# A hybrid decoder block on one core: value products, their sum, and the gates' second half move within the units of the mix stage, and four attention blocks start a unit later

## The chip, the cores and the metric

The kernel runs on one core of a Trainium2 chip. The metric is the device time of one execution in microseconds (us); the figure for a kernel is the median of its runs. TensorE (PE) does the matrix products, VectorE (DVE), ScalarE (ACT) and GpSimd (POOL) the elementwise work, SyncE (SP) issues the weight loads. Each engine works through its own queue in order and waits there for what it needs from others.

## The reference

One decoder block over 512 tokens and 16 learned meta tokens, width 1024, in float32: a SwiGLU, then attention and a state-space layer side by side, merged by sigmoid gates, then a second SwiGLU.

```python
h = h + 0.5 * swiglu(rmsnorm(h, ffn1_norm), w1, w3, w2)
q, k, v, u, g_attn, g_ssm = jnp.split(rmsnorm(h, mix_norm) @ w_in, SPLITS, axis=-1)
attn = sliding_window_attention(q, k, v, attn_sinks)   # 16 heads, 4 of keys and values, window 128, 16 meta keys, a sink per head
y = jax.nn.gelu(s5_ssm(u, ...))
ssm = (y @ ssm_glu_a) * jax.nn.sigmoid(y @ ssm_glu_b)
merged = jax.nn.sigmoid(g_attn) * attn + jax.nn.sigmoid(g_ssm) * ssm
h = h + merged @ w_out
h = h + 0.5 * swiglu(rmsnorm(h, ffn2_norm), ...)
return rmsnorm(h, final_norm)[:, N_META:]
```

## The kernel before

Activations lie transposed, features on partitions and the 512 tokens along the row. Every float32 operand of a large product is split into a high and a low part (`hi`, `lo`), and each product is done as three: hi by hi, hi by lo, lo by hi. The weights come in by SP's queue, are split by ACT (`whi`, L173) and DVE (`wlo`, L174), and are used a *unit* at a time: a unit is one tile of 128 output columns, 8 chunks of 128 rows by three products, so 24 matmuls of 128x512 (L238) into one PSUM bank.

The change lies in the mix stage, 30 units that stand in the order of the table `MIX`: the remaining query columns (`q`), the gates of attention (`ga`) and of the state-space layer (`gs`), and the two halves of its output (`glu`, "value-gate units": a unit with two banks, 12 products for the half `b`, then 12 for `a`). Unit 4 is the first `glu`, unit 9 the second `ga`, unit 15 the last `q`.

The attention runs between the products of these units. It is cut into 16 blocks b0 to b15: block n is key head n // 4 with 128 query rows n % 4, four query heads at once. A block takes three units:

- `s1` in its first unit, once for each of four heads: a *score pair* on PE (L1167, L1168, into one of two score banks), the masked minimum on DVE (L1170: writes `E`, `mn` and frees the bank), the exp on ACT (L1172). After the fourth head come the sums `den` on DVE, and POOL multiplies `E` by 1/`den` (L1183).
- `s2o`, `s2p`, `s2m` in the next unit: PE transposes `E` (L1191), ACT and DVE split it (`ph`, `pl`); the meta keys' part is transposed (L1210), split into `ms`, and POOL spreads it over the heads as `m` (`m4` in the code, L1215).
- `s3` in the third unit: the *value products* (L1226, four, or two where n % 4 is 0) into the only value bank `pv`; `s3m`: the *sum product* with the meta values (L1234), which needs `m`; `s3e`: the *sum of the halves*, hi part and lo part of the values: ACT copies one half (`tb`, L1240), DVE adds the other into `AT` (L1242, twice), which frees the bank.

Where each of these stands in a unit is written by hand. A unit of 24 products has 11 cuts: cut j comes before product 2(j + 1). In a `glu` unit cuts 0 to 5 fall into the first half (before its products 1, 3, 5, 6, 8, 10) and 6 to 10 into the second (before 2, 4, 6, 8, 10). `BEGIN` holds the unit in which each block starts, `CUT` the cut of each step. What a unit leaves in its bank is taken up at cut 0 of the next (`flush`). The next weight tile is prepared at cut 8 (`prep_piece`). No scheduler changes this order afterwards: the engines' queues are filled as the code runs.

```python
if i - 2 in begin:
    for f, c in ((s3, "s3"), (s3m, "s3m"), (s3e, "s3e")):
        at_cut(CUT[c], f, begin[i - 2])
if i in begin:
    for h in range(4):
        at_cut(CUT["s1"][h], s1, begin[i], h)
if i - 1 in begin:
    for f, c in ((s2o, "s2o"), (s2p, "s2p"), (s2m, "s2m")):
        at_cut(CUT[c], f, begin[i - 1])
```

Of the kernel before, what the change touches and what calls it, by code (L numbers as in the profile page):

```python
# [10 lines left out]
AF = mybir.ActivationFunctionType  # L11
ALU = mybir.AluOpType
# [25 lines left out]
PREPS = (6, 34)  # L38
KS1 = 8
VS = (1, 0, 2, 10, 13, 13)  # L40
CUT = {"s3": 5, "s3m": 7, "s3e": 9, "s1": (2, 4, 7, 7), "s2o": 7, "s2p": 7, "s2m": 8, "prep": 8, "ev": 0, "ks": 10, "vs": 7}
BEGIN = (1, 2, 3, 4, 6, 7, 10, 11, 13, 14, 15, 18, 19, 20, 21, 24)

NG = 32
NST = 64
# [20 lines left out]
def hybrid_block_kernel(  # L66
# [30 lines left out]
    V, S, G, PE, SY = nc.vector, nc.scalar, nc.gpsimd, nc.tensor, nc.sync  # L97
# [13 lines left out]
    def real(t):  # L111
        return t.rearrange("p (h c) -> p h c", h=2)[:, :, :256]
# [79 lines left out]
    def step(mm, evac, hold=False, mids=(), prep=True):  # L192
        hi, lo = take()
        mm(hi, lo, mids)
        if prep:
            prep_piece()
        pend.append(evac)
        if not hold:
            flush()
# [31 lines left out]
    def mm3(outs, hi, lo, rhi, rlo, nk, mids, k0=0):  # L231
        seq = []
        for k in range(nk):
            seq += [(hi, rhi, k), (hi, rlo, k), (lo, rhi, k)]

        def emit(w, r, k, start, stop):
            for o, sl in outs:
                PE.matmul(out=o, lhsT=w[:, k0 + k, :], rhs=sl(r, k), start=start, stop=stop)  # L238

        accumulate(seq, emit, mids)  # L240
# [10 lines left out]
    def mm512(ps, hi, lo, rhi, rlo, nk, mids, k0=0, packed=True):  # L251
        if packed:
            mm3([(ps, lambda r, k: r[:, k, :])], hi, lo, rhi, rlo, nk, mids, k0)
        else:
            mm3([(ps, lambda r, k: real(r[:, k, :]))], hi, lo, rhi, rlo, nk, mids, k0)
# [48 lines left out]
    def new_hg(cols=COLS, p=hg_p):  # L304
        hi = p.tile([128, ND, cols], F32R, tag="hgh", name="hgh")
        lo = p.tile([128, ND, cols], F32R, tag="hgl", name="hgl")
        return hi, lo
# [720 lines left out]
    def h2(t):  # L1028
        return t.rearrange("p (h c) -> p h c", h=2)

    def unit512(evac_f):
        cell = {}

        def mm(hi, lo, mids):
            cell["p"] = mm_ps.tile([128, 512], F32, tag="mm", name="p")
            mm512(cell["p"], hi, lo, hg[0], hg[1], ND, mids, packed=False)
        return mm, lambda: evac_f(h2(cell["p"]))
# [47 lines left out]
    AT = a_p.tile([128, ND, SEQ], F32, name="AT")  # L1085
# [4 lines left out]
    def tmp(name):  # L1090
        return a_p.tile([128, 512], F32, tag="t", name=name, bufs=4)
# [157 lines left out]
    def merge(m):  # L1249
        V.scalar_tensor_tensor(out=AT[:, m, :], in0=gst.pop(m), scalar=0.5, in1=AT[:, m, :], op0=ALU.mult, op1=ALU.add)  # L1250
        if m >= 6:
            msplit(m)

    def ev_ga(m):
        def f(p):
            t = tmp("ta")
            V.tensor_tensor(out=h2(t), in0=p, in1=r512, op=ALU.mult)
            S.activation(out=t, in_=t, func=AF.Tanh, scale=0.5)
            V.scalar_tensor_tensor(out=AT[:, m, :], in0=t, scalar=1.0, in1=AT[:, m, :], op0=ALU.add, op1=ALU.mult)
            if m < 6:  # L1260
                merge(m)
        return f

    def ev_gs(m):
# [7 lines left out]
    def unit_glu(m):  # L1272
        cell = {}

        def mm(hi, lo, mids):
            n = (len(mids) + 1) // 2
            for key, k0, ms in (("b", 4, mids[:n]), ("a", 0, mids[n:])):
                cell[key] = mm_ps.tile([128, 512], F32, tag="mm", name="p")
                mm512(cell[key], hi, lo, YH, YL, 4, ms, k0)

        def ev():
            t = tmp("tg")
            S.activation(out=t, in_=cell["b"], func=AF.Tanh, scale=0.5)
            V.scalar_tensor_tensor(out=t, in0=t, scalar=1.0, in1=cell["a"], op0=ALU.add, op1=ALU.mult)
            V.scalar_tensor_tensor(out=gst[m], in0=gst[m], scalar=1.0, in1=t, op0=ALU.add, op1=ALU.mult)
            if m >= 6:
                merge(m)
        return mm, ev
# [3 lines left out]
    def msplit(m):  # L1292
        S.activation(out=mg[0][:, m, :], in_=AT[:, m, :], func=AF.Copy)
        V.tensor_tensor(out=mg[1][:, m, :], in0=AT[:, m, :], in1=fr(mg[0][:, m, :]), op=ALU.subtract)
# [5 lines left out]
    for kind, r in MIX:  # L1300
        for m in (2 * r, 2 * r + 1):
            units.append(unit_glu(m) if kind == "glu" else unit512({"q": ev_q, "ga": ev_ga, "gs": ev_gs}[kind](m)))
    begin = dict(zip(BEGIN, range(16)))
    for i, u in enumerate(units):
        cuts = [[] for _ in range(NCUT)]

        def at_cut(c, f, *a):
            cuts[c].append(lambda: f(*a))
# [8 lines that stand above are left out]
            for f, c in ((s2o, "s2o"), (s2p, "s2p"), (s2m, "s2m")):  # L1317
                at_cut(CUT[c], f, begin[i - 1])
        at_cut(CUT["ev"], flush)
        if i == KS1:  # L1320
            at_cut(CUT["ks"], ksplit, 1)
            at_cut(CUT["ks"], vmeta, 1)
        for v, iv in enumerate(VS):
            if i == iv:
                at_cut(CUT["vs"], vsplit, *divmod(v, 3))
        at_cut(CUT["prep"], prep_piece)
        if i == len(units) - 2:
            mg += new_hg(SEQ)
            for m in range(6):
                at_cut(m, msplit, m)  # L1330

        step(*u, mids=[lambda fs=fs: [f() for f in fs] for fs in cuts], prep=False, hold=i < len(units) - 1)
# [170 lines left out]
```

## Time and profile before

| | |
|---|---|
| median of 3 runs | 1147.18 us (1145.42 to 1149.43) |
| the profiled execution | 1148.62 us, its span 1146.80 us |
| busy in the span: PE, PE weight loads | 1127.8 us (98%), 1006.2 us (88%) |
| busy: DVE, ACT, POOL | 636.5 (55%), 410.4 (36%), 357.1 us (31%) |
| chain that ended last | PE 88%, DVE 5%, ACT 4%, issue 2%, DMA 1% |
| matmuls in L238 | 403.6 + 403.1 + 401.2 us, 1408 of each kind |

A row of the profile in order of time reads: start, duration, engine, line, operation, output <- inputs, shape, and in brackets how long the engine had been idle and what ended that. Matmuls overlap, so their spacing and not their duration tells PE's pace. A row of the waits reads: engine and operation that waited, what it waited for, us in total, times, the longest. A row of stretches has the stretch, its length, the busy time of PE, its weight loads, DVE, ACT and POOL, then the granted clock of PE, the DMA share and GB/s.

### The profile page before, as it was taken

The page shows a single profiled execution, that of the slowest core. Times are in us where ns is not written, and L with a number is a line of the kernel's source. Part 1 is how long each engine was busy: PE and PEld are TensorE (multiplying, and loading weights), DVE is VectorE, ACT ScalarE, POOL GpSimd, SP SyncE. Part 2 cuts the span into 40 slices and gives each one's busy share as a digit, 9 for nine tenths or more (in the row PEclk, how much of TensorE's full clock was granted, in tenths as well). Part 3 has the DMA queues.
Part 4 walks back from the last instruction along what each step waited for, and adds up shares of the span by engine and source line. Part 5 has one row for each costly group of instructions (what it writes and reads, how often), then busy time and mean ns, then how long its engine had stood idle before and what let it go on. Part 6 is the DMA issues. An engine that isn't in the chain of part 4 may idle for free.

```text
span 1146.8 us, 17241 instructions
## 1 busy us (share of the span) xinstructions
PE 1127.8 (98%) x7006; PEld 1006.2 (88%) x7006; DVE 636.5 (55%) x960; ACT 410.4 (36%) x727; POOL 357.1 (31%) x488
## 2 busy tenths in 40 slices
PE   9999999999999999999999999999999999999997
PEld 7999999999999999977778778888888888888887
DVE  5446663655444464867767776664544444444454
ACT  5322232232222242465646554443322321322234
POOL 1966663542883030444444231020000000000003
PEclk7999999999999999999999999999999999999999
DMA  5423233232423246212211222432423224313222
GB/s 164 115 94 110 74 94 112 75 85 84 112 87 95 77 160 170 56 63 74 74 58 53 74 74 81 144 106 74 129 92 111 74 83 127 111 65 128 75 74 74
DMA packets 105583, 108.43 MB, mean 95 GB/s; under 512 B 7504, under 2 KB 101968, under 8 KB 105376
## 3 DMA queue, kind: packets, MB, share of 16 engines
q1 hardware_dynamic: 103104, 100.74, 28.0%
q0 software_dynamic: 2352, 6.52, 2.2%
q8 instruction: 55, 0.90, 0.3%
q14 instruction: 24, 0.20, 0.1%
q10 hardware_dynamic: 48, 0.07, 0.0%
HBM read 100.80 MB, written 5.34 MB: 93 GB/s over the span
## 4 chain that ended last, share of the span: by engine, by line
PE 88%; DVE 5%; ACT 4%; issue 2%; DMA 1%; POOL 0%; SPq 0%; DVEq 0%; POOLq 0%; ACTq 0%
PE p L238 59%; PE p L412 11%; PE p L414 9%; PE p L800 2%; PE pv L1226 1%; PE p L1398 1%; DVE wlo L174 1%; ACT whi L173 1%; PE ps_t L1191 1%; DVE AT L1242 1%; PE ps_s L1167 1%; ACT E L1172 1%; PE ps_s L1168 1%; DMA xb<-in_x_dram 1%; ACT qs L1144 0%
## 5 line engine op out<-in xcount | busy, mean ns | idle before, releaser
L238 PE MATMUL p<-hgh,whi 128*128 128x264 f32 (+1 forms) x1408 | 403.6, 333 | 0.1
L238 PE MATMUL p<-hgl,whi 128*128 128x264 f32 (+1 forms) x1408 | 403.1, 332 | 0.0
L238 PE MATMUL p<-hgh,wlo 128*128 128x264 f32 (+1 forms) x1408 | 401.2, 331 | 0.0
L174 DVE TENSOR_TENSOR wlo<-raw,whi 128x1024 fp32r<-128x1024 f32 (+2 forms) x192 | 257.7, 1342 | 91.6 <-ACT whi L173 89.4
L238 PEld LDWEIGHTS p<-hgh,whi 128*128 128x128 f32 x1408 | 238.9, 188 | 26.0 <-issue 0.8
L238 PEld LDWEIGHTS p<-hgh,wlo 128*128 128x128 f32 x1408 | 238.6, 189 | 23.5
L238 PEld LDWEIGHTS p<-hgl,whi 128*128 128x128 f32 x1408 | 238.9, 188 | 22.4
L173 ACT ACTIVATE whi<-raw 128x1024 fp32r<-128x1024 f32 (+2 forms) x192 | 187.5, 979 | 133.5 <-PE p L414 72.2
L1414 POOL TENSOR_TENSOR acc<-acc,zq 128x256 f32<-128x256 f32 x12 | 8.9, 738 | 349.8 <-ACT zq L1407 349.7
L432 DVE SCALAR_TENSOR_TENSOR hT<-p,hT 128x528 f32<-128x528 f32 (+1 forms) x56 | 39.1, 698 | 87.1 <-PE p L414 52.2
L384 ACT ACTIVATE t<-t 128x528 f32<-128x528 f32 (+1 forms) x44 | 28.1, 639 | 165.0 <-DVE t L383 164.9
L394 ACT ACTIVATE gh<-t 128x528 fp32r<-128x528 f32 (+1 forms) x44 | 28.1, 639 | 160.6 <-DVE t L393 160.6
L412 PE MATMUL p<-gh,whi 128*128 128x264 f32 x352 | 72.6, 288 | 0.7 <-DVE hT L432 0.5
L412 PE MATMUL p<-gl,whi 128*128 128x264 f32 x352 | 71.5, 284 | 0.0
L412 PE MATMUL p<-gh,wlo 128*128 128x264 f32 x352 | 71.4, 284 | 0.0
L383 DVE TENSOR_TENSOR t<-p,r_bc 128x528 f32<-128x528 f32 (+1 forms) x44 | 30.7, 698 | 71.3 <-PE p L238 68.1
L393 DVE TENSOR_TENSOR t<-p,t 128x528 f32<-128x528 f32 (+1 forms) x44 | 30.7, 698 | 65.4 <-PE p L238 65.0
L412 PEld LDWEIGHTS p<-gh,whi 128*128 128x128 f32 x352 | 54.5, 189 | 1.9 <-issue 0.8
L414 PE MATMUL p<-gh,whi 128*128 128x512 f32 x144 | 56.0, 389 | 0.0
L414 PE MATMUL p<-gl,whi 128*128 128x512 f32 x144 | 56.0, 389 | 0.0
L414 PE MATMUL p<-gh,wlo 128*128 128x512 f32 x144 | 56.0, 389 | 0.0
L385 DVE TENSOR_TENSOR t<-t,r_bc 128x528 f32<-128x528 f32 (+1 forms) x44 | 37.2, 846 | 32.4 <-ACT t L384 32.4
(322 smaller groups left out, 1502.2 us busy)
## 6 DMA issues: line engine op xcount, KB each, us to landing
raw<-in_ffn_w_dram SPq DMA_DIRECT2D x42, 1024.0 KB, 5.4
raw<-in_ffn_w_dram SPq DMA_DIRECT2D x24, 768.0 KB, 4.3
raw<-in_w_in_dram SPq DMA_DIRECT2D x16, 1024.0 KB, 5.5
raw<-in_ffn_w_dram SPq DMA_DIRECT2D x12, 512.0 KB, 3.6
raw<-in_w_out_dram SPq DMA_DIRECT2D x4, 1024.0 KB, 8.1
h_keep<-hT POOLq DMA_DIRECT2D x1, 2112.0 KB, 7.3
raw<-in_ssm_glu_a_dram SPq DMA_DIRECT2D x4, 512.0 KB, 3.6
raw<-in_ssm_glu_b_dram SPq DMA_DIRECT2D x4, 512.0 KB, 5.3
```

The source lines that it names most:

```text
L173: S.activation(out=hi, in_=src, func=AF.Copy)
L174: V.tensor_tensor(out=lo, in0=src, in1=fr(hi), op=ALU.subtract)
L238: PE.matmul(out=o, lhsT=w[:, k0 + k, :], rhs=sl(r, k), start=start, stop=stop)
L383: V.tensor_tensor(out=t1, in0=cell[1], in1=rb(), op=ALU.mult)
L384: S.activation(out=t1, in_=t1, func=AF.Silu)
L385: V.tensor_tensor(out=t1, in0=t1, in1=rb(), op=ALU.mult)
L393: V.tensor_tensor(out=t3, in0=cell[3], in1=cell["t1"], op=ALU.mult)
L394: S.activation(out=gh, in_=t3, func=AF.Copy)
L412: PE.matmul(out=p[:, h, :HALF], lhsT=wt[:, k, :], rhs=gs[k][c][:, h, :], start=start, stop=stop)
L414: PE.matmul(out=p, lhsT=wt[:, k, :], rhs=gs[k][c].rearrange("p h c -> p (h c)"), start=start, stop=stop)
L432: V.scalar_tensor_tensor(out=hv(hT, d), in0=cell["p"], scalar=0.5, in1=hv(hT, d), op0=ALU.mult, op1=ALU.add)
L800: PE.matmul(out=p[:, h, :HALF], lhsT=w[:, k, :], rhs=r[:, k, h * HALF:(h + 1) * HALF], start=(n == 0), stop=(n == 3 * ND - 1))
```

## The change

The value products go from cut 5 to cut 1, the sum product from 7 to 3, the sum of the halves from 9 to 5. The second half of an attention gate (two DVE operations, L1259 and L1250) no longer follows its first half at cut 0 but is kept back (`pend2`) to cut 6. The tanh of a value-gate unit is issued as soon as its half `b` is done, no longer with the rest at the next unit's cut 0. Blocks b0 to b3 start in units 2 to 5 in place of 1 to 4; the other twelve stay.

```diff
-CUT = {"s3": 5, "s3m": 7, "s3e": 9, "s1": (2, 4, 7, 7), ...}
-BEGIN = (1, 2, 3, 4, 6, 7, 10, 11, 13, 14, 15, 18, 19, 20, 21, 24)
+CUT = {"s3": 1, "s3m": 3, "s3e": 5, "ev2": 6, "s1": (2, 4, 7, 7), ...}
+BEGIN = (2, 3, 4, 5, 6, 7, 10, 11, 13, 14, 15, 18, 19, 20, 21, 24)
...
+    pend2 = []
+
+    def flush2():
+        while pend2:
+            pend2.pop(0)()
...
     def ev_ga(m):
...
             S.activation(out=t, in_=t, func=AF.Tanh, scale=0.5)
-            V.scalar_tensor_tensor(out=AT[:, m, :], in0=t, scalar=1.0, in1=AT[:, m, :], op0=ALU.add, op1=ALU.mult)
-            if m < 6:
-                merge(m)
+
+            def second():
+                V.scalar_tensor_tensor(out=AT[:, m, :], in0=t, scalar=1.0, in1=AT[:, m, :], op0=ALU.add, op1=ALU.mult)
+                if m < 6:
+                    merge(m)
+            pend2.append(second)
...
     def unit_glu(m):
...
                 mm512(cell[key], hi, lo, YH, YL, 4, ms, k0)
+                if key == "b":
+                    t = cell["t"] = tmp("tg")
+                    S.activation(out=t, in_=cell["b"], func=AF.Tanh, scale=0.5)
 
         def ev():
-            t = tmp("tg")
-            S.activation(out=t, in_=cell["b"], func=AF.Tanh, scale=0.5)
+            t = cell["t"]
...
         at_cut(CUT["ev"], flush)
+        at_cut(CUT["ev2"], flush2)
```

In the queues, the numbers behind the names tell one buffer from another. PE in unit 15, where b10 is scored, b9 transposed and b8 summed, before: around b8's value products and sum product.

```order
L1167 MATMUL ps_s_6892<-KH_5678,qs_6264 128x272
L1168 MATMUL ps_s_6892<-KL_5679,qs_6264 128x272
L238 MATMUL p_6865<-hgl_213,whi_6769 128x512
L238 MATMUL p_6865<-hgh_212,wlo_6770 128x512
L1226 MATMUL pv_6899<-ph_6842,VB_5680 128x512
L1226 MATMUL pv_6899<-pl_6843,VB_5680 128x512
```

And after, the same products of the same block:

```order
L238 MATMUL p_6865<-hgh_212,whi_6775 128x512
L1226 MATMUL pv_6877<-ph_6842,VB_5680 128x512
L1226 MATMUL pv_6877<-pl_6843,VB_5680 128x512
L238 MATMUL p_6865<-hgl_213,whi_6775 128x512
L238 MATMUL p_6865<-hgh_212,wlo_6776 128x512
L1167 MATMUL ps_s_6886<-KH_5678,qs_6254 128x272
L1168 MATMUL ps_s_6886<-KL_5679,qs_6254 128x272
```

Before, two score pairs and 12 products of the unit stand ahead of the value products; after, 4 products and no pair. The sum product follows four products later in both.

DVE in the same unit, before: the end of b10's scores (`E` and `mn` of the fourth head), the rest of its unit, and then b8's sum of the halves.

```order
L1170 ISA E_6879,mn_6880<-ps_s_6912,mC_5684,sinkn_67 128x272
L1170 ISA mn_6880 128x1
L1175 TENSOR_TENSOR es_6882<-mn_6880,sinkn_67 128x4
L1177 TENSOR_TENSOR den_6881<-den_6881,es_6882 128x4
L1178 RECIPROCAL den_6881<-den_6881 128x4
L1181 TENSOR_TENSOR pm_6921<-E_6879,den_6881 128x64
L1195 TENSOR_TENSOR pl_6931<-ps_t_6925,ph_6930 128x512
L1195 TENSOR_TENSOR pl_6940<-ps_t_6934,ph_6939 128x512
L1213 TENSOR_TENSOR ms_6947<-ps_tm_6945,ms_6947 64x128
L174 TENSOR_TENSOR wlo_6953<-raw_6623,whi_6952 128x1024
L1242 TENSOR_TENSOR AT_5682<-pv_6899,tb_6961 64x2x128 x2
```

And after, from the second head's score on:

```order
L1170 ISA E_6882,mn_6883<-ps_s_6896,mC_5684,sinkn_67 128x272
L1170 ISA mn_6883 128x1
L1242 TENSOR_TENSOR AT_5682<-pv_6877,tb_6903 64x2x128 x2
L1170 ISA E_6882,mn_6883<-ps_s_6911,mC_5684,sinkn_67 128x272
L1170 ISA mn_6883 128x1
```

The additions into `AT` went from behind `wlo`, the last work of the unit, to between the second and the third head's score.

POOL at b2 to b4, before: `E` times 1/`den` of a block (L1183), then `m` of the block ahead of it (L1215).

```order
L1183 TENSOR_TENSOR E_6024<-E_6024,den_6026 128x4x256
L1215 TENSOR_TENSOR m4_6098<-ms_6095,hm_5685 128x512
L1215 TENSOR_TENSOR m4_6167<-ms_6164,hm_5685 128x512
L1183 TENSOR_TENSOR E_6196<-E_6196,den_6198 128x4x128
L1145 TENSOR_TENSOR qs_6264<-tq_6262,qs_6264 64x512 x2
```

And after:

```order
L1183 TENSOR_TENSOR E_6063<-E_6063,den_6065 128x4x256
L1215 TENSOR_TENSOR m4_6138<-ms_6135,hm_5685 128x512
L1183 TENSOR_TENSOR E_6166<-E_6166,den_6168 128x4x128
L1215 TENSOR_TENSOR m4_6237<-ms_6234,hm_5685 128x512
L1145 TENSOR_TENSOR qs_6254<-tq_6252,qs_6254 64x512 x2
```

With b3 scored in unit 5 and b4 in unit 6, `E` of b4 now stands ahead of `m` of b3.

More of the change, by code (lines that the diff above doesn't have):

```diff
@@ L40 @@
 VS = (1, 0, 2, 10, 13, 13)
-CUT = {"s3": 5, "s3m": 7, "s3e": 9, "s1": (2, 4, 7, 7), "s2o": 7, "s2p": 7, "s2m": 8, "prep": 8, "ev": 0, "ks": 10, "vs": 7}
-BEGIN = (1, 2, 3, 4, 6, 7, 10, 11, 13, 14, 15, 18, 19, 20, 21, 24)
+CUT = {"s3": 1, "s3m": 3, "s3e": 5, "ev2": 6, "s1": (2, 4, 7, 7), "s2o": 7, "s2p": 7, "s2m": 8, "prep": 8, "ev": 0, "ks": 10, "vs": 7}
+BEGIN = (2, 3, 4, 5, 6, 7, 10, 11, 13, 14, 15, 18, 19, 20, 21, 24)
 NG = 32
```

## The prediction, as it was put on record

> **What bounds the kernel now.** I read the page's first part, then the waits of TensorE (PE), then the mix stage (units 0 to 29, about 498 to 728 us) as a table of stretches, then its rows in order of time. PE is the bound; its idle time is what a reordering can move.
>
> ```profile
> PE 1127.8 (98%) x7006; PEld 1006.2 (88%) x7006; DVE 636.5 (55%) x960; ACT 410.4 (36%) x727; POOL 357.1 (31%) x488
> PE ps_s L1167 <- DVE mn L1170: 4.5, 4, 2.0
> PE pv L1226 <- DVE AT L1242: 4.1, 8, 0.9
> 582.00:584.30 2.30, 0.27 (x2) 0.00 (x0) 1.86 (x5) 0.39 (x2) 0.00 (x0) 1.00 1.00 335
> 584.30:588.70 4.40, 4.40 (x14) 3.59 (x15) 3.08 (x12) 3.64 (x11) 1.51 (x2) 0.61 0.10 35
> 504.00:513.00 9.00, 7.46 (x37) 5.64 (x36) 5.11 (x13) 6.23 (x10) 8.39 (x6) 1.00 0.00 0
> ...
> 510.43 0.31 PE L1167 MATMUL ps_s<-KH,qs 128*128 128x144 f32 x1 [1.54 <-DVE mn L1170]
> 530.20 0.39 PE L238 MATMUL p<-YH,wlo 128*128 128x512 f32 x1
> 530.43 0.39 PE L238 MATMUL p<-YH,whi 128*128 128x512 f32 x1
> ...
> 541.20 0.39 PE L238 MATMUL p<-YH,whi 128*128 128x512 f32 x1
> ...
> 542.50 0.47 PE L1226 MATMUL pv<-ph,VB 128*128 128x512 f32 x1 [0.91 <-DVE AT L1242]
> 586.30 0.63 PE L238 MATMUL p<-hgh,whi 128*128 128x512 f32 x1
> 586.72 0.63 PE L238 MATMUL p<-hgl,whi 128*128 128x512 f32 x1
> ```
>
> Four waits of a score pair for a free score bank and eight of the value products for the one value bank hold 4.5 + 4.1 = 8.6 us. A wait costs more than its bracket: 541.20 to 542.50 is 1.30 where products follow each other by 0.23 (530.20, 530.43), so 0.16 beside the 0.91; twelve waits make 1.9. After the longest (2.04 us, unit 10) the granted clock is 0.61 for 4.4 us: eight products at 0.42 in place of 0.23, 1.6 us; after 1.54 us in unit 1 the clock stayed at 1.00. With 0.2 for the one wait of L1234 on m (shown further on), 12.3 us can go, 1.1% of the span. PE's instructions are the same, so nothing else can.
>
> **What the change removes.** The value bank is freed by the two AT additions. They come at cut 9 of a unit, behind that unit's wlo on VectorE (DVE), and the next value products at cut 5 of the next. Now they come at cut 5, ahead of wlo, and the products that need them at cut 1 of the next unit, more than 4 us later: all eight waits (4.1) go. Of the score waits, unit 10's comes from DVE's queue:
>
> ```profile
> 580.09 0.84 DVE L1242 TENSOR_TENSOR AT<-pv,tb 64x256 f32<-64x256 f32 x2
> 580.96 0.69 DVE L1257 TENSOR_TENSOR ta<-p,r_bc 128x512 f32<-128x512 f32 x1
> 582.41 0.69 DVE L1259 SCALAR_TENSOR_TENSOR AT<-ta,AT 128x512 f32<-128x512 f32 x1 [0.76 <-ACT ta L1258]
> 583.14 0.69 DVE L1250 SCALAR_TENSOR_TENSOR AT<-ts,AT 128x512 f32<-128x512 f32 x1
> 583.75 0.49 DVE L1170 CUSTOM_DVE_ANT_0 E<-ps_s,mC,sinkn 128x272 f32<-128x272 f32 x1
> ```
>
> Of these, AT (0.84), the tanh gap (0.76) and both gate halves (1.4) leave the place ahead of the first score: 3.0 us against a wait of 2.04, so it goes, and the slow stretch with it. The waits of units 1 and 2 belong to blocks that move one unit on, where no late exps stand ahead of wlo; the fourth (unit 14) is, with unit 2's, what 1.54 and 2.04 leave of 4.5, so under 0.9, against AT's 0.84 that leaves its place too. All 12.3 go. The tanh of the value gate, issued between the halves, I cost at nothing: it stands on ScalarE (ACT) after tb and ahead of exps that wait for DVE anyway; bare, it would be one 0.60 us. No DMA moves to another queue; GpSimd (POOL) keeps its work in nearly the same order.
>
> **What it adds: the sum product meets POOL.** The product that ends the sum (L1234) needs m, which POOL spreads (L1215) after it has multiplied the next block's E by den (L1183), if that block was scored in the same unit. Block b1 today:
>
> ```profile
> 526.40 0.29 PE L1167 MATMUL ps_s<-KH,qs 128*128 128x272 f32 x1
> 526.86 0.50 DVE L1170 CUSTOM_DVE_ANT_0 E<-ps_s,mC,sinkn 128x272 f32<-128x272 f32 x1 [0.57 <-PE ps_s L1168]
> 526.91 1.04 PE L1191 MATMUL ps_t<-ident,E 128*128 128x128 f32 x8
> 527.40 0.52 ACT L1172 ACTIVATE E<-E,mn 128x272 f32<-128x272 f32 x1 [0.27 <-DVE mn L1170]
> 527.92 0.51 ACT L1172 ACTIVATE E<-E,mn 128x272 f32<-128x272 f32 x1
> 529.20 2.04 POOL L1183 TENSOR_TENSOR E<-E,den 128x512 f32<-128x512 f32 x2 [3.44 <-ACT ph L1194]
> 529.75 0.39 PE L238 MATMUL p<-YH,whi 128*128 128x512 f32 x1
> 530.83 1.49 DVE L174 TENSOR_TENSOR wlo<-raw,whi 128x1024 fp32r<-128x1024 f32 x1
> 531.19 2.03 POOL L1215 TENSOR_TENSOR m<-ms,hm 128x512 fp32r<-128x512 f32 x1
> 535.60 0.39 PE L1234 MATMUL pv<-m,VM 128*128 128x512 f32 x1
> ```
>
> Read it as one chain: third score pair at 526.40, DVE takes it at 526.86 (+0.46), exps, sums, E times den from 529.20, m from 531.19 to 533.22: 6.36 us after 526.86. L1234 comes 2.4 us later. Three other cases:
>
> ```profile
> 560.34 0.50 DVE L1170 CUSTOM_DVE_ANT_0 E<-ps_s,mA,sinkn 128x272 f32<-128x272 f32 x1 [0.19 <-PE ps_s L1168]
> 565.32 2.02 POOL L1215 TENSOR_TENSOR m<-ms,hm 128x512 fp32r<-128x512 f32 x1
> 566.93 0.39 PE L238 MATMUL p<-hgh,whi 128*128 128x512 f32 x1
> 567.40 0.50 PE L1234 MATMUL pv<-m,VM 128*128 128x512 f32 x1
> 655.04 0.37 DVE L1170 CUSTOM_DVE_ANT_0 E<-ps_s,mC,sinkn 128x144 f32<-128x144 f32 x1 [0.25 <-PE ps_s L1168]
> 658.91 2.08 POOL L1215 TENSOR_TENSOR m<-ms,hm 128x512 fp32r<-128x512 f32 x1 [0.72 <-DVE ms L1213]
> 672.61 0.50 DVE L1170 CUSTOM_DVE_ANT_0 E<-ps_s,mC,sinkn 128x272 f32<-128x272 f32 x1 [0.47 <-PE ps_s L1168]
> 676.95 2.02 POOL L1215 TENSOR_TENSOR m<-ms,hm 128x512 fp32r<-128x512 f32 x1
> ```
>
> In the other cases with E ahead of m the lag from the third score's row lies between 5.95 (655.04 to 660.99, behind a narrow block, 144 wide) and 7.0 (560.34 to 567.34, where query copies hold ACT), mostly 6.2 to 6.4 (the last of them 672.61 to 678.97). That POOL's row is real shows at b4, the one place where PE waits for it today: m ends at 567.34, L1234 starts at 567.40, 0.24 later than one product after 566.93.
>
> The new order lets L1234 come 8 products earlier (cut 3 in place of 7), 10 in a value-gate unit: 1.9 to 2.3 us, and one score pair (0.26). The slack is eaten. Per block: m is ready 0.46 + lag + 0.06 after the third pair; PE reaches L1234 after two pairs (0.51), eight transposes and what follows to the unit's end (526.91 to 529.75, 2.84; about 2.4 with four), then in the next unit 8 products (1.86; 6, 1.39, in a value-gate unit), value products (four 0.93, two 0.46) and a score pair if one is due (0.26). For b1: 0.51 + 2.84 + 1.39 + 0.93 + 0.26 = 5.93 against 6.88: PE waits 0.95. So for b0 to b4: 1.7, 0.95, 0.4, 0.2, 1.5; b6 1.1; b8 1.2; b9 0.7; b11 0.7; b12 1.7; b13 0.7: 11.0 us in eleven waits (b5, b7, b10, b14, b15 have no E ahead of m, and none). b3 is new among them: with the first blocks a unit later, b4 is scored in its unit.
>
> **The waits feed each other.** AT now stands between the second and third score on DVE, and AT waits for tb, which on ACT stands behind the second exp. From the second score on DVE: exp after 0.54 (526.86 to 527.40), 0.52, tb 0.60, AT 0.84 (the exps' rows are above):
>
> ```profile
> 540.27 0.60 ACT L1240 ACTIVATE tb<-pv 64x512 f32<-64x512 f32 x1
> 541.52 0.84 DVE L1242 TENSOR_TENSOR AT<-pv,tb 64x256 f32<-64x256 f32 x2
> ```
>
> with handovers 2.56 us, so the third score starts on DVE 3.0 after the second pair began on PE, not 1.65 + 0.46 = 2.1 (in a value-gate unit 2.1 + 0.46 = 2.57). That adds 0.9 (0.45; 0.7 narrow) to the lag of every block whose m is made in a unit that also sums: b1, b2, b12, b13 0.45 each, b3 0.7, b4 and b9 0.9: 4.3 us. From below: nothing, if PE is late anyway.
>
> **The sum.** -12.3 + 11.0 + 4.3 = +3.0 us, on a profiled execution of 1148.62 (span 1146.80 and 1.82 around it): 1151.6. That run was 1.44 above the median of the runs shown, so I predict 1147.18 + 3.0 = **1150.2**. With the bounds 0 and 4.3 for the feedback it is 1145.9 to 1150.2. About 0.3% (3.4 us) is what a measurement of this kernel can tell from no change: 1143.7 to 1150.6.
>
> **Rivals.** *POOL's spread goes ahead of wlo (faster).* DVE's wlo and m obstruct each other: where m came first it took 1.04 and wlo paid.
>
> ```profile
> 548.13 1.04 POOL L1215 TENSOR_TENSOR m<-ms,hm 128x512 fp32r<-128x512 f32 x1 [5.63 <-DVE ms L1213]
> 548.15 2.10 DVE L174 TENSOR_TENSOR wlo<-raw,whi 128x1024 fp32r<-128x1024 f32 x1
> ```
>
> If the new order brings m there first in all eleven, each lag is 1.0 shorter; of 15.3 us 4.9 stay (the short waits vanish whole): -12.3 + 4.9, 1139.8. Against it: today wlo is first wherever E times den stands ahead. It decides if the new waits sum to under 8.9.
>
> *The clock falls again (slower).* Waits of b4 (2.4) and b12 (2.2) exceed the 2.04 after which 1.6 us were lost: 3.2 more, 1153.4. Against it: value products that wait for pl break those waits in two, and 1.54 us cost nothing. By the Trainium skill (TensorE: Matmul & The Clock Gate, Part 1: The HAM clock gate) the clock halves only after an idle window of some 3.4 us; by that page no wait here would do it, and the sum would stay 1150.2. The trace disagrees: 2.04 us sufficed, so I keep the rival.
>
> *No feedback.* The new waits pay back what went: -12.3 + 11.0, 1145.9. *They are all hidden:* 1134.9; only if POOL's rows were wrong, which 567.34 to 567.40 speaks against; I give it 2 in 100, inside the first rival.
>
> **Chances.** Forecast (1148.5 to 1152.0) 0.42; POOL first 0.17; clock 0.26; no feedback 0.15. Faster by over 0.3%: 0.17 and 0.03 of the last: 0.20. Of the forecast's band 0.6 lies below 1150.6: within 0.3%: 0.25 + 0.12 = 0.37. Slower: 0.17 + 0.26 = 0.43. The range, 1141.5 to 1155.0, leaves out half of the first rival and a third wait that slows the clock; the likeliest's own range is 1148.5 to 1152.0.
>
> **What would show it.** In the profile after, PE's waits of L1226 for AT and of L1167 for mn are under 1 us together, and L1234 waits for POOL's m about eleven times, 13 to 16 us by start-to-start, longest at b4 and b12. DVE shows AT idle until tb, and the third score right behind it. Unit 10 is shorter by about 3.8 us (2.04 + 0.16 + 1.6). I am wrong if L1234's waits stay under 9 us (then it is faster), if L1226 waits for pl instead, or if wlo comes too late for the next unit's weights.

## The result, and the profile after

| | before | after |
|---|---|---|
| median of the runs of one comparison (9 each) | 1149.42 us (1145.42 to 1151.92) | 1155.75 us (1151.86 to 1156.93) |
| ratio | | 1.0053, 95% interval 1.0036 to 1.0069 |
| the profiled execution, its span | 1148.62, 1146.8 us | 1153.12, 1151.3 us |
| mix stage, start of unit 0 to end of unit 29 | 229.14 us | 234.66 us |
| outside it | 917.7 us | 916.7 us |

The change makes the kernel half a per cent slower, and the loss lies in the mix stage (+5.5 us). First the page after: PE's part, PE's waits in the stage (line that waits, what it waits for, us in total, times, longest), and the chain that ended last.

```profile
PE 1125.6 (98%) x7006; PEld 1002.3 (87%) x7006; DVE 635.4 (55%) x960; ACT 411.2 (36%) x727; POOL 358.7 (31%) x488
PE pv L1234 <- POOL m L1215: 11.9, 11, 1.7
PE ps_s L1167 <- DVE mn L1170: 2.0, 2, 1.1
PE ps_tm L1210 <- DVE mn L1170: 0.5, 1, 0.5
PE 82%; DVE 6%; ACT 5%; POOL 4%; issue 2%; DMA 0%; DVEq 0%; POOLq 0%; ACTq 0%; SPq 0%
```

PE is as busy as before, in a longer span. The eight waits of the value products for AT are gone, and of the score waits two are left; in their place stand eleven waits of the sum product for POOL's m, where before a single one came 0.24 us late (the row at 567.40 in the prediction). New as well is one wait of tm, the transpose of the meta keys' part (L1210). POOL has entered the chain with 4%, and PE's share of it fell from 88 to 82.

The chain of waits in units 5 and 6 (start, length, what) shows how such a wait arises:

```profile
538.40 0.50 PE pv L1234
...
539.64 0.50 DVE E L1170
...
540.19 0.61 ACT E L1172 x2
...
540.83 0.60 ACT tb L1240
...
541.46 0.42 DVE AT L1242
...
541.89 0.42 DVE AT L1242
...
542.34 0.50 DVE E L1170
...
542.88 0.64 ACT E L1172 x3
...
544.09 0.49 ACT ph L1194
...
544.67 1.67 POOL E L1183
...
546.52 2.03 POOL m L1215
...
548.60 0.50 PE pv L1234
```

It starts at one sum product and ends at the next, 10.20 us later, and only 1.2 us of it are PE's own work. The sum product of b1 is followed by the second score on DVE, its exp, then tb and AT of b1, and behind them the third score of b3; then exps, E times den, m of b2, and the sum product of b2. This is a ring: it goes round once per unit, and as long as its steps take what they take here, a unit in which it is closed cannot be shorter than the ring is long, whatever PE has to do. Units 4 to 8 last 9.2 to 10.3 us each, 48.9 together. PE itself needs less: in e8 below, which has the change without its value part, the same five last 43.0 us together, waits of 1.7 included.

### The profile page after: what moved, and what is told of

Same layout as the page of the kernel before. It is cut to its first block, busy times and chain, and to the rows that moved or that the text cites. A ratio compares the mean times of both kernels' runs of the same rounds, so it can differ in the third digit from the quotient of the medians.

```text
span 1151.3 us, 17230 instructions
## 1 busy us (share of the span) xinstructions
PE 1125.6 (98%) x7006; PEld 1002.3 (87%) x7006; DVE 635.4 (55%) x960; ACT 411.2 (36%) x727; POOL 358.7 (31%) x488
## 4 chain that ended last, share of the span: by engine, by line
PE 82%; DVE 6%; ACT 5%; POOL 4%; issue 2%; DMA 0%; DVEq 0%; POOLq 0%; ACTq 0%; SPq 0%
PE p L238 55%; PE p L412 11%; PE p L414 9%; POOL m L1215 2%; ACT E L1172 2%; POOL E L1183 1%; PE p L800 1%; DVE wlo L174 1%; PE p L1410 1%; DVE E L1170 1%; ACT whi L173 1%; PE ps_x L746 1%; DVE AT L1242 1%; PE pv L1234 1%; ACT tb L1240 0%
## 5 line engine op out<-in xcount | busy, mean ns | idle before, releaser
L1183 POOL TENSOR_TENSOR E<-E,den 128x512 f32<-128x512 f32 (+1 forms) x20 | 28.5, 1431 | 94.7 <-DVE den L1178 49.7
```

The lines of the kernel that those rows point to most:

```text
L1183: G.tensor_tensor(out=E[:, :, c:c + w], in0=E[:, :, c:c + w], in1=den.unsqueeze(2).to_broadcast([128, 4, w]), op=ALU.mult)
```

## The experiments

Eighteen kernels, each timed against the kernel before in the same comparison. "Cuts" are those of value products, sum product and sum of the halves; "m" that of the meta part (s2m); "late gates" the gates' half put off, with the tanh between the halves (e3 without this tanh). The stage is that of the profiled execution; in before, e7, e17 and e18 it holds one stretch of 3.4 us at a granted clock of 0.50 (last section), which costs about 1.6 us, as the prediction worked out for before.

| kernel | cuts, m | first block in unit | late gates | ratio to before (95%) | stage, us |
|---|---|---|---|---|---|
| before | 5, 7, 9; 8 | 1 | no | 1 | 229.1 |
| after | 1, 3, 5; 8 | 2 | yes | 1.0053 (1.0036 to 1.0069) | 234.7 |
| e1_begin | 5, 7, 9; 8 | 2 | no | 0.9988 (0.9977 to 1.0000) | 226.4 |
| e2_value | 1, 3, 5; 8 | 1 | no | 1.0076 (1.0061 to 1.0090) | 237.1 |
| e3_gates | 5, 7, 9; 8 | 1 | yes | 0.9977 (0.9964 to 0.9989) | 225.8 |
| e4_spread_early | 1, 3, 5; 0 | 2 | yes | 1.0040 (1.0026 to 1.0055) | 231.4 |
| e5_at_early | 1, 3, 4; 8 | 2 | yes | 1.0045 (1.0030 to 1.0059) | 233.6 |
| e6_scale_behind | 1, 3, 5; 8 | 2 | yes | 1.0033 (1.0020 to 1.0045) | 231.4 |
| e7_spread_mid | 1, 3, 5; 5 | 2 | yes | 1.0048 (1.0034 to 1.0062) | 235.4 |
| e8_value_back | 5, 7, 9; 8 | 2 | yes | 0.9969 (0.9958 to 0.9979) | 224.9 |
| e9_spread_bank | 1, 3, 5; 3 | 2 | yes | 1.0082 (1.0068 to 1.0096) | 238.8 |
| e10_table_early | 5, 7, 9; 8 | 2 | yes | 0.9987 (0.9975 to 0.9998) | 224.6 |
| e11_value_half | 3, 5, 7; 8 | 2 | yes | 1.0020 (1.0009 to 1.0030) | 229.7 |
| e12_begin_three | 5, 7, 9; 8 | 3 | yes | 0.9955 (0.9941 to 0.9969) | 223.9 |
| e13_sum_behind | 5, 7, 8; 8 | 3 | yes | 0.9922 (0.9903 to 0.9941) | 218.5 |
| e14_half_behind | 3, 5, 8; 8 | 2 | yes | 0.9937 (0.9916 to 0.9958) | 221.5 |
| e15_after_behind | 1, 3, 8; 8 | 2 | yes | 1.0035 (1.0021 to 1.0049) | 232.2 |
| e16_best | 3, 5, 8; 8 | 3 | yes | 0.9933 (0.9919 to 0.9947) | 220.3 |
| e17_sum_only | 5, 7, 8; 8 | 1 | no | 0.9935 (0.9919 to 0.9950) | 223.5 |
| e18_value_only | 3, 5, 8; 8 | 1 | no | 0.9979 (0.9965 to 0.9992) | 226.7 |

**The parts one by one.** e1 has only the blocks' shift, e2 only the value part, e3 only the gates' late half.

```diff
# e1, against before
-BEGIN = (1, 2, 3, 4, 6, 7, 10, ...
+BEGIN = (2, 3, 4, 5, 6, 7, 10, ...
# e2, against before
-"s3": 5, "s3m": 7, "s3e": 9
+"s3": 1, "s3m": 3, "s3e": 5
# e3, against before
+"ev2": 6    # and pend2, flush2 and ev_ga's second() of the change
```

> The kernel before with only the start of b0 to b3 one unit later. Queue theory (the time lies in PE's waits for m behind POOL's and DVE's queue, which come only when the sum product stands early): nearly no change, -1 to +2 us. The score waits of units 1 and 2 (2.6 us by start-to-start before) come back in units 2 and 3 as in the changed kernel (2.3), L1234 waits for m at most once or twice and under 1 us in all, and unit 5, now scoring too, adds one or two waits of L1226 for AT of 0.5 to 1 us. Rival (the six blocks in a row overload DVE, and that is the loss): +4 us or more, with L1226 or L1167 waiting in units 4 to 8.

> The kernel before with only the cuts of the value products, the sum product and the sum of the halves at 1, 3 and 5. Queue theory: L1226's waits for AT (5.4 us by start-to-start) go, L1234 waits for m ten or eleven times, 12 to 14 us by start-to-start, ps_tm about 1; unit 10's score wait shrinks by AT's 0.84 and its slow clock may stay. Sum +6 to +9 us against before, ratio 1.005 to 1.008: this part alone makes the loss. Rival (the loss comes from the other parts): no change or a gain, -4 to +1 us.

> The kernel before with only the second half of the attention gates kept back to cut 6. Queue theory: unit 10's score wait (2.04 us) and the slow clock after it (1.6 us) go, nothing else changes: -3 to -4 us, ratio 0.9965 to 0.9975, L1234 waits no more than before. Rival (the two gate operations ahead of the third score delay den, E and m): unit 10's wait goes but L1167 or L1234 waits as long elsewhere, no change within 1 us.

e2 alone has the whole loss, in the upper half of what was expected. The other two parts gain: e1 1.4 us by the ratio, a little past its theory's 1 us, with an interval that reaches to no change; of the 2.7 us by which its stage is shorter, 1.6 are the slow clock, which happens to be absent there. e3 gains a little less than foretold by the ratio (2.6 us; its stage is 3.4 shorter). The wait of e2 that the kernel before has not:

```profile
PE pv L1234 <- POOL m L1215: 11.9, 10, 1.7
```

In e3 unit 10 lost its wait and its slow stretch: it lasts 7.12 us in place of 10.84, as the prediction had it (7.16 in the changed kernel).

**The value part put back.** e8 is the changed kernel without its value part.

```diff
-"s3": 1, "s3m": 3, "s3e": 5
+"s3": 5, "s3m": 7, "s3e": 9
```

> The changed kernel with the three cuts of the value part put back (s3, s3m, s3e at 5, 7, 9): the first blocks' shift, the gates' late half and the earlier glu tanh stay. Theory (the parts add up): the gains of e1 (-0.12%) and e3 (-0.23%) sum to a ratio of 0.996 to 0.997 of the kernel before, L1234 waits for m under 1 us, and AT waits of about 4 us remain. Rival (the gains of e1 and e3 are the same wait counted twice): 0.998 to 0.999.

The parts add up: 0.9969 against the product of e1 and e3, 0.9965. (No run moves the tanh between the halves alone; what it can add or take here is within these intervals.) So the value part costs 1.0053 to 0.9969, 0.8%, some 9.7 us, within the change.

**Taking m's wait away.** If the loss were m's lateness, an earlier m would cure it. e4 and e7 move the meta part (tm, ms, m) to other cuts of the block's second unit; e9 also gives tm a bank of the transposes' pool. tm reads pm, the meta keys' columns of E times 1/den, which DVE makes after the fourth score (L1181).

```diff
# e4, against after      # e7: 5
-"s2m": 8
+"s2m": 0
# e9, against after
-"s2m": 8
+"s2m": 3
-ps = sc_ps.tile([128, 512], F32, tag="sc", name="ps_tm")
+ps = pt_ps.tile([128, 512], F32, tag="pt", name="ps_tm")
```

> The changed kernel with the meta part's transposition, split and spread (L1210, ms, m) at cut 0 in place of 8: on POOL m then stands ahead of the multiplication of E and is ready most of a unit before the sum product. Queue theory: L1234 waits for m not at all (11.9 us by the waits, 13.7 by start-to-start, in the changed kernel), ps_tm's waits (1.1) go too, at most 1 us of new waits of L1226 for pl: -13 us against the changed kernel, about 1142, ratio to before 0.992 to 0.996. Rival (the waits on m only show what DVE's scores make late, and PE waits for pl or for AT in its place): within 3 us of the changed kernel, ratio 1.003 to 1.007, L1226 waiting 8 to 12 us for pl.

> The changed kernel with tm, ms and m (s2m) at cut 5 of the next unit in place of cut 8 of the same unit's numbering, so behind pm and ahead of the late E times den. In e4, with s2m at cut 0, the waits for m went and waits for pm of 8.6 us came, since pm is ready about 2 us into the unit. Theory (what the early value products lack is only a place for tm between pm and the end of the unit): L1234 waits for m under 1 us, L1210 for pm under 1 us, and the stage is 12 to 14 us shorter than with the change: ratio to the kernel before 0.991 to 0.995. Rival (the score banks: tm now takes one between the second and the third score): the third score or its successor waits for ms, as in e4 (1.3 us there), 3 us or more in sum, ratio 0.997 to 1.000. Second rival (the engines' lateness only moves on, to wlo and the next unit's weights): ratio 1.000 or above.

> The changed kernel with s2m moved to cut 3 of the next unit and its transpose tm put into a bank of the transposes' pool (pt) in place of the scores' (sc). In e4 (cut 0) tm waited for pm, 8.6 us; in e7 (cut 5) the third score waited for the bank that tm held, 8.9 us, and tm for the score ahead of it, 4.9 us. Theory (with pm ready and a bank of its own nothing is left that m or tm hold up): PE's waits for m, pm and ms are under 1.5 us together, the stage is 11 to 14 us shorter than with the change, and the ratio to the kernel before is 0.991 to 0.995. Rival (DVE and ACT are late with the scores themselves: in the units that score, the first score is evacuated 4.5 us after the unit's start): L1167's waits for mn grow to 5 us or more and the ratio is 0.996 to 0.999. Second rival (the lateness passes to AT or to wlo again): 1.000 or above.

I expected a gain of 11 to 14 us three times and was wrong three times. PE's waits in the stage, for e4, e7 and e9 in this order:

```profile
PE ps_tm L1210 <- DVE pm L1181: 8.6, 9, 1.6
PE ps_s L1167 <- DVE ms L1213: 1.3, 3, 0.8
```

```profile
PE ps_s L1167 <- DVE ms L1213: 8.9, 11, 2.1
PE ps_tm L1210 <- DVE mn L1170: 4.9, 5, 1.8
```

```profile
PE ps_s L1167 <- DVE mn L1170: 9.7, 11, 1.4
...
PE ps_t L1191 <- DVE ms L1213: 1.9, 3, 1.0
```

The waits for m (11.9) are gone in all three, and each time others stand elsewhere: 9.9, 13.8 and 11.6 us in these lines, in e9 another 4.2 of the value products for ph and pl. Only e4's stage is clearly shorter than with the change, by 3.2 us. In e4 tm comes before pm is ready. In e7 tm holds a score bank until ms has read it, and ms stands on DVE behind AT. In e9 pm and the scores' bank are out of the way (tm now holds a bank of the transposes, for the 1.9), and the third score itself is late, behind tb and AT; as its chain of waits in unit 5 has it, from the second score to the third:

```profile
542.22 0.50 DVE E L1170
...
542.76 0.62 ACT E L1172 x2
543.39 0.60 ACT tb L1240
...
544.02 0.42 DVE AT L1242
...
544.90 0.50 DVE E L1170
```

**m's place on POOL, and AT ahead of the second score.** e6 issues E times den behind m; e5 moves the sum of the halves one cut forward.

```diff
# e6, against after
-    for c, w in ...: G.tensor_tensor(out=E[...], in0=E[...], in1=den..., op=ALU.mult)   # in s1
+    # the same loop as a step of its own, s1e, at cut 9, behind s2m
# e5, against after
-"s3e": 5
+"s3e": 4
```

> The changed kernel with POOL's E times den (L1183) issued behind m in place of ahead of it; nothing else moves. Theory (POOL's own queue holds m): m comes 1.0 to 1.3 us earlier per block, of 13.7 us of waits of L1234 some 3 to 4 stay, the ratio to the kernel before is about 0.995 to 0.997. Rival (it is DVE's wlo, which holds POOL's work wherever it stands in the queue): m comes 0.3 us earlier per block, L1234 still waits 10 to 11 us, the ratio is 1.002 to 1.004.

> The changed kernel with one number more: the sum of the halves (tb, AT) stands ahead of the second score pair (cut 4) instead of behind it (cut 5), so that AT no longer stands between the second and the third score on DVE. Theory (the feedback of the prediction): m's lag shrinks by up to 4.3 us over seven blocks; PE's waits of L1234 for m fall from 13.7 to 9 to 10 us, the tm waits (1.1) go, and the ratio to the kernel before comes down from 1.005 to about 1.001. Rival (no feedback; the delay of the third score is PE's own lateness): the waits of L1234 stay at 13 to 14 us and the ratio stays at 1.005. Second rival: AT, moved ahead, makes the second score late instead; L1234's waits shrink and L1167 waits for mn by as much, ratio 1.004 to 1.006.

e6 came out near its rival. First in POOL's queue was not enough: wlo was there 0.05 us ahead and m took 2.07 (DVE and POOL in unit 5 of e6):

```profile
537.93 1.23 DVE L174 TENSOR_TENSOR wlo<-raw,whi 128x1024 fp32r<-128x1024 f32 x1
537.98 2.07 POOL L1221 TENSOR_TENSOR m<-ms,hm 128x512 fp32r<-128x512 f32 x1 [6.18 <-DVE ms L1219]
```

PE's waits for m fell from 11.9 to 8.3 us, further than the rival has it, and the stage by 3.3; the ratio is the rival's. In e5, whose waits are next, those for m fell by 3.2 us, as the feedback of the prediction has it, and the scores' waits rose by 2.6, which is its second rival:

```profile
PE pv L1234 <- POOL m L1215: 8.7, 10, 1.7
PE ps_s L1167 <- DVE mn L1170: 4.6, 7, 1.0
```

The stage moved by 1.0. AT ahead of the second score still stands ahead of the third.

**AT behind the scores.** e11 takes the value part half-way back; e14 differs from e11 in one number, the place of tb and AT: ahead of the third score there, behind the fourth here. e15 does the same to the changed kernel.

```diff
# e11, against after
-"s3": 1, "s3m": 3, "s3e": 5
+"s3": 3, "s3m": 5, "s3e": 7
# e14, against e11
-"s3e": 7
+"s3e": 8
# e15, against after
-"s3e": 5
+"s3e": 8
```

> The changed kernel with the value part's cuts at 3, 5, 7, halfway between before (5, 7, 9) and the change (1, 3, 5). Theory (PE's wait for m is m's lag less the products ahead of L1234; two cuts later are 0.9 to 1.0 us more ahead): of 13.7 us of waits of L1234 about 3 us stay, in b0, b1, b4, b12; the waits of L1226 for AT (4.2 in e8) go, since AT stands ahead of the third score; the third score is late by up to 0.8, which brings 2 to 4 us of waits of L1167 or L1234. Ratio to the kernel before 0.995 to 0.999, near that of e8. Rival (the waits scale with the cuts): half the loss, 7 us of waits for m, ratio 1.000 to 1.002.

> e11 (the value part at 3, 5, 7) with the sum of the halves behind the fourth score (cut 8) in place of ahead of the third (cut 7); the value products stay. Loop theory (what AT ahead of the third score costs is a ring over DVE and ACT, which shows at whatever PE waits for next): of e11's 5.0 us of waits of tm for mn and 2.9 of L1234 for m at most 2 us stay together; L1226 waits for AT now by 0.2 to 0.5 in ten units, 2 to 4 us; ratio to the kernel before 0.995 to 0.998, against 1.002 for e11. Rival (the place of L1234 alone makes the loss): the waits for m stay at 3 us or grow, the waits for AT come on top, ratio 1.001 or above.

> The changed kernel with the sum of the halves at cut 8 in place of 5, so behind the fourth score; value products and the sum product stay at cuts 1 and 3. It opens the same ring in the changed kernel itself, but the bank of pv then comes free about 1.6 us into the next unit, where L1226 wants it after 0.5 to 0.9. Loop theory: the period of a dense unit falls from 9.6-10.4 to 9.0-9.6, the waits for m fall under 5 us, L1226 waits for AT 5 to 9 us in ten units; ratio to the kernel before 0.999 to 1.003. Rival (the waits for m do not depend on AT): m's 13.7 us stay beside the waits for AT, ratio 1.006 or above.

PE's waits in the stage, e11 and then e14:

```profile
PE ps_tm L1210 <- DVE mn L1170: 5.0, 7, 1.2
PE pv L1234 <- POOL m L1215: 2.9, 6, 0.7
PE ps_s L1167 <- DVE mn L1170: 2.4, 3, 1.1
```

```profile
PE ps_s L1167 <- DVE mn L1170: 2.2, 3, 1.1
PE pv L1234 <- POOL m L1215: 1.0, 3, 0.5
```

e11 came out at its rival's upper end (1.0020) and not where its theory had it: the waits for m fell as foretold, but 5.0 us of waits of tm came that neither had. From e11 to e14 one number took 8.2 us off the stage, with the sum product in its early place, more than the theory gave (0.9937 against 0.995 to 0.998). The tm waits went whole (the third score frees tm's bank), m's to a third, and the waits for AT that I had expected did not come. The chain of e14 in units 5 to 7 is PE's own:

```profile
544.31 0.93 PE pv L1226 x4
...
547.96 0.89 PE ps_t L1191 x8
...
549.41 2.79 PE p L238 x12
```

Units 4 to 8 last 42.5 us in it, against 46.8 in e11 and 48.9 after the change. In e15 the same number brought only 2.5 us, and the ratio lies just above its theory's range:

```profile
PE pv L1234 <- POOL m L1215: 5.3, 9, 1.3
PE pv L1226 <- DVE AT L1242: 3.7, 7, 0.8
```

The waits for m halved, but with value products at cut 1 AT behind the scores frees their bank too late, and another ring closes (pl, AT, value products, sum product, scores, pl: in its chain of waits 9.25 us from pl at 543.51 to pl at 552.76). So the two places work together: against the changed kernel AT behind the scores alone gives 2.5 us, all three steps two cuts later (e11) 5.0, both 13.1.

**What holds the first units.** Two waits stayed at the stage's start. e10 is e8 with a tiny exponential in unit 1, to load ACT's table earlier; e12 is e8 with the first six blocks one unit later once more.

```diff
# e10, against e8
+if i == 1:
+    at_cut(8, warm)     # S.activation(out=t, in_=sinkn[:, 0:4], func=AF.Exp)
# e12, against e8
-BEGIN = (2, 3, 4, 5, 6, 7, 10, ...
+BEGIN = (3, 4, 5, 6, 7, 8, 10, ...
```

> e8 (the change without its value part) with one tiny exponential (128 x 4) issued on ACT in unit 1, where ACT is idle, so that the load of ACT's table (1.28 us, ahead of the first exp of b0) is over before it is needed. Theory (the waits of units 2 and 3 that came back are ACT's backlog at the start of the stage, and the one in unit 3, 0.87, is the table's load): the wait in unit 3 falls to 0.2 or less, the one in unit 2 (1.10) stays, the stage is 0.7 to 0.9 shorter than e8's; the ratio to e8 is too small for the timing, so the profile decides. Rival (both waits stem from the query copies and the splits of the weights): unit 3's wait stays at 0.7 to 0.9.

> e8 with the first six blocks one unit later once more (units 3 to 8 in place of 2 to 7). Theory (backlog at the stage's start): the wait of unit 2 (1.10, query copies, V copy and weight split ahead of tq) goes; in the first unit that scores, none or under 0.3 stays, but the table's load still makes the second one wait, 0.6 to 0.9; ratio to the kernel before 0.995 to 0.998. Rival (it moves with the first block, wherever that stands): 1.1 and 0.9 in units 3 and 4. Second rival: b5, now in a gate unit (8) beside b4's sum, brings new waits of 1 us or more there, and the ratio is that of e8 or higher.

In e10 the wait of unit 3 went, as the theory has it, but unit 2's grew from 1.10 to 2.07: I had put the load between the V copy and whi, and ACT was not idle there. Moving a cost within a queue that is full moved the wait; the stage stayed (224.6 against 224.9; by the ratios, of two comparisons, e10 is if anything slower). In e12 two waits stayed, of 0.40 and 0.36: less than the rival has, though the first is more and the second less than the theory gave. They shrink when the first block stands later, so most of them is the backlog at the stage's start. The stage is 1.0 shorter than e8's.

**A version to keep.** e13 is e12 with AT one cut earlier, behind the fourth score but ahead of wlo. e17 does that alone to the kernel before; e18 adds the early value products to e17; e16 is e14 with e12's first blocks.

```diff
# e17, against before; e13, against e12
-"s3e": 9
+"s3e": 8
# e18, against e17
-"s3": 5, "s3m": 7
+"s3": 3, "s3m": 5
```

> e12 with the sum of the halves (tb, AT) one cut earlier, at 8: still behind the fourth score, but ahead of ms and wlo on DVE, where e12 has it behind wlo. Loop theory (where AT stands behind the scores it closes no ring between DVE and ACT, and what is left in e12 is AT's end behind wlo, 4.0 us of waits of L1226): these waits go, nothing new comes, the stage is 3 to 4 us shorter than e12's; ratio to the kernel before 0.991 to 0.993. Rival (AT delays ms and m by 0.85 and wlo by as much, and DVE's lateness returns as waits for mn or hgl): 1.5 to 3 us come back, ratio 0.994 to 0.997.

> The kernel before with one number changed: the sum of the halves at cut 8 in place of 9, so AT ahead of ms and wlo on DVE. Theory (before's 4.1 us of waits of L1226 are AT's place behind wlo, nothing else): these waits go, the scores' waits (4.5, unit 10's 2.0 among them) stay; ratio 0.996 to 0.997. Rival (AT ahead of wlo makes wlo and the next unit's first score late): L1167's waits grow by 2 us or more, ratio 0.998 or above.

> The kernel before with the value part alone, at 3, 5, 8 instead of the change's 1, 3, 5 (e2, which had 1.0076). Theory (the value products may go two cuts earlier as long as the sum stays behind the fourth score): L1226's waits for AT under 1 us, L1234's for m 1 to 1.5 us, ratio 0.996 to 0.998, not better than e17. Rival (early value products lose wherever the sum stands): 1.000 or above.

> e14 (value part at 3, 5, sum of halves at 8, gates' late half) with the first six blocks in units 3 to 8 as in e12 and e13. Loop theory: with no ring closed, the value products' place is worth nothing more; what is left in e14 (2.2 us of waits for mn at the start, 1.0 for m) shrinks to about 2 us in sum as in e13: ratio to the kernel before 0.991 to 0.9935, the same as e13 within the intervals. Rival (the early value products are a gain of their own): 0.990 or below. Second rival (b5 in a gate unit and the early L1234 make new waits for m): 0.994 or above.

e13 does what was foretold, 0.9922: 0.6 to 1.0% faster than before, with a stage 5.4 us shorter than e12's, more than the 3 to 4 expected. Of PE's waits in its stage only this line is over 0.2 us in all:

```profile
PE ps_s L1167 <- DVE mn L1170: 1.5, 3, 0.7
```

e17 shows that one number of the kernel before brings most of this (0.9935): its waits of L1226 for AT are gone. In before AT starts behind wlo, in the same unit (the row at 541.52 in the prediction; first line here), in e17 ahead of it (the others):

```profile
540.33 1.26 DVE L174 TENSOR_TENSOR wlo<-raw,whi 128x1024 fp32r<-128x1024 f32 x1
```

```profile
538.16 1.28 DVE L1195 TENSOR_TENSOR pl<-ps_t,ph 128x512 fp32r<-128x512 f32 x2
539.36 0.84 DVE L1242 TENSOR_TENSOR AT<-pv,tb 64x256 f32<-64x256 f32 x2
540.12 0.27 DVE L1213 TENSOR_TENSOR ms<-ps_tm,ms 64x128 fp32r<-64x128 f32 x1
540.44 1.23 DVE L174 TENSOR_TENSOR wlo<-raw,whi 128x1024 fp32r<-128x1024 f32 x1
```

It gained more than I expected (0.6% against 0.3 to 0.4); I had counted the eight waits by their brackets (4.1 us), where by start-to-start they hold 5.4, and the stage is 5.7 us shorter. e18 against e17, and e16 against e13, show that early value products are no gain of their own: 0.9979 against 0.9935, a loss, and 0.9933 against 0.9922 (from two comparisons, with intervals that overlap), no difference.

## Why the prediction was right and where it was wrong

The direction was right (slower had 0.43), and so was the mechanism that I gave for it: PE waits for m in exactly the eleven blocks foretold, b3 among them, longest in b12 and b4 (1.73 and 1.66). The forecast of +3.0 us was too small; the stage grew by 5.5, and 1155.75 lies above the range's 1155.0. Of the distance from 1150.2, 2.2 us are the starting point: in the same comparison the kernel before stood at 1149.42, and the prediction counts from 1147.18. The rest, 3.3, is the change: 6.3 us by the medians against +3.0. The steps of the sum that failed are "All 12.3 go", of which 2.6 us came back, and the transpose tm, which the sum has at nothing and which waits for 1.1 us. Step by step:

- *All eight waits for AT go (4.1).* Right: none is left.
- *Unit 10 is shorter by about 3.8.* Right: 10.84 to 7.16, and e3 shows that the gates' late half does it. The 1.6 us of slow clock in that sum are not always there, though: e1 has the same wait (2.08) and no slow stretch (last section).
- *"The waits of units 1 and 2 belong to blocks that move one unit on, where no late exps stand ahead of wlo."* This step failed. They came back in units 2 and 3 with 1.10 and 0.88, start to start 2.3 us, in the changed kernel as in e1, which has the shift alone. ACT and DVE in unit 2 of the changed kernel:

```profile
508.01 1.28 ACT L1144 ACTIVATE qs<-tq 64x512 fp32r<-64x512 f32 x2 [2.61 <-DVE tq L1151]
509.31 0.38 ACT L1128 ACTIVATE VB<-ps_v 128x256 fp32r<-128x256 f32 x1
509.72 1.06 ACT L173 ACTIVATE whi<-raw 128x1024 fp32r<-128x1024 f32 x1
512.37 0.68 DVE L1151 SCALAR_TENSOR_TENSOR tq<-p,r_bc 128x512 f32<-128x512 f32 x1
512.97 0.35 DVE L1170 CUSTOM_DVE_ANT_0 E<-ps_s,mC,sinkn 128x144 f32<-128x144 f32 x1
514.38 1.28 ACT L1172 ACT_TABLE_LOAD   x1
515.68 0.42 ACT L1172 ACTIVATE E<-E,mn 128x144 f32<-128x144 f32 x1
```

  In unit 2 not exps but query copies and a V copy stand ahead of whi, wlo waits for whi, and the first score for wlo. In unit 3 there are late exps after all: the load of ACT's table stands ahead of them (with the load moved ahead, in e10, that wait is gone). I had looked for late exps because they stood there before, and had not asked what else ACT does in these units.
- *The sum product meets POOL, 11.0, and the feedback, 4.3.* Together 15.3 (the eleven terms of the first add up to 10.85); by start-to-start the waits for m sum to 13.7, each within 0.6 us of its forecast. So as sizes they are close, and they do not make the miss. What the prediction did not see is what stands behind the feedback, which it has as a longer lag of m, paid once in seven blocks. AT ahead of the third score closes a ring, and its length comes out at whatever PE waits for first: m (after), pm (e4), the scores' bank (e7), mn (e9). That is why an earlier m did not cure the loss: by the stage a third of it went in e4, next to none in e7 and none in e9. The waits of tm for mn, 1.1 us, may be a piece of the ring; no run shows them apart. With AT behind the scores and the value products at 3 and 5, nearly all of it is gone (e14).
- *The sum.* -12.3 + 13.7 (m) + 2.6 (score waits that came back, 0.3 of it in unit 19) + 1.1 (tm) = +5.1, of the 5.5 that the stage grew; 0.4 stays unexplained. So the terms that were too small, 2.6 and 1.1, outweigh the one that was too large by 1.6. The profiled spans differ by 4.5, the medians by 6.3, the interval reaches from 4.1 to 7.9.
- *POOL's spread first.* Did not come: the new waits sum to over 8.9. e6 shows that the queue's order would not have brought it either: m first in POOL's queue still lost to wlo. What decides is which of wlo and m starts first.
- *The clock falls again.* Did not come: the granted clock is 1.00 throughout the stage after. The longest waits were 1.8 to 1.9 us start to start, not 2.2 to 2.4, so the rival's condition was never met. Its rule, by the length of the wait, does not hold either (last section).
- *No feedback, all hidden.* The second fell with the eleven waits. The first fell with e15: AT behind the scores alone takes the waits for m from 11.9 to 5.3 us.

The largest gain that one number brought over the kernel before lay in a row of the prediction's first fence, which I read only as a wait that would go: before's waits for AT come from AT's place behind wlo, and one cut earlier they are gone (e17).

## What to carry to other kernels

When an edit puts work on which an engine waits between two steps of a chain that comes round with every unit, follow the chain until it meets itself: if it does, its length is the floor of the unit, and taking away one of its waits does not shorten the unit. A wait that is taken away and comes back elsewhere with about the same size is the sign of such a ring; look in the chain of waits for what all versions have in common, here tb and AT ahead of the third score. Work whose result is wanted late belongs behind the steps on which the ring turns and ahead of the long ones that nobody waits for yet, and one number of the order can be worth more than an earlier start of the product.

## What the hardware showed

*Two waits of the same length, two clocks.* In before PE's wait of 2.04 us in unit 10 is followed by a granted clock of 0.50; in e1 a wait of 2.08 us at the same place is followed by full speed. The traces show why. In before the clock is 0.50 from 585.14 to 588.56, for 3.41 us, and the changes of the clock that its trace records lie 13.65, 563.20, 3.41 and 552.96 us apart: 4, 165, 1 and 162 times 3.413. In the other traces too they lie such multiples apart. Cut into windows on this grid (us, PE busy, PE weight loads, DVE, ACT, POOL, granted clock, DMA), before and then e1 read:

```profile
581.73:585.14 3.41, 1.37 (x8) 0.82 (x7) 2.51 (x7) 1.49 (x4) 0.00 (x0) 1.00 0.87 280
585.14:588.56 3.42, 3.42 (x11) 2.75 (x10) 2.28 (x10) 2.80 (x9) 1.37 (x2) 0.50 0.00 0
```

```profile
577.90:581.32 3.42, 2.44 (x12) 1.69 (x10) 2.58 (x6) 0.63 (x1) 0.53 (x1) 1.00 0.47 134
581.32:584.73 3.41, 2.31 (x12) 1.97 (x13) 2.56 (x10) 2.33 (x9) 0.00 (x0) 1.00 0.49 174
```

The wait of before lies whole in one window and leaves PE busy for 1.37 us of it; that of e1 is split over two, with 2.44 and 2.31. In the mix stages of all these traces four windows have PE busy for 1.4 us or less (1.37 here, 1.29 in e7, 1.08 in e18, 1.01 in e17), and each of the four, and no other, is followed by one window at 0.50; the least busy of the others has 1.68 (in the changed kernel, from 670.80). So it is not the wait's length that decides but how much of one window it takes, and for a wait of 2 us that depends on where it falls. The Trainium skill (TensorE: Matmul & The Clock Gate, Part 1: The HAM clock gate) says that PE's activity is watched in a window of 3413 ns that runs freely, whatever the kernel does, which agrees. The same section has the clock fall after an idle window; here a window with 1.37 us of work in it sufficed.

*The table load.* 1.28 us ahead of the first exponential (514.38 above), and the exponential starts 0.02 us behind its end, at 515.68. The Trainium skill (ScalarE: Activation LUTs, What ACT_TABLE_LOAD costs) gives 1283 ns for the load, which agrees, and a drain of some 1380 ns on top, which these rows do not show.

*wlo and m.* Of these two, whichever starts first takes its short time (wlo 1.23, m 1.04), and the other takes 2.07 to 2.10: 0.02 to 0.05 us decide (before at 548.13, e6 at 537.93).
